# Nine tiles of a modulation as row products on VectorE in the dense layer

## The chip, the cores and the metric

The kernel runs on one core of one Trainium2 chip. A time is the device time of one execution of the whole program in microseconds, and a change is judged by the median of several executions. A profiled execution gives the span (first to last instruction) and a trace of every engine: TensorE (PE, with its weight loads as PEld), VectorE (DVE), ScalarE (ACT), GpSimd (POOL) and SyncE (SP), whose queue issues nearly all transfers.

## The reference, cut to what matters

Two layers work on 256 latent and 256 context tokens of 1024 features, all in fp32. Both layers take shifts, scales and gates from a conditioning vector `c` and from a fixed context vector `c_ctx`:

```python
s_c, s_cc = silu(c), silu(c_ctx)
for l in range(2):
    sh1, sc1, gt1, sh2, sc2, gt2 = split(s_c @ w_ada[l] + b_ada[l], 6)      # latent tokens
    sh1c, ..., gt2c              = split(s_cc @ w_ada[l] + b_ada[l], 6)     # context tokens
    h = rmsnorm(x) * (1 + sc1) + sh1
    x = x + gt1 * (mixer(h @ w_in[l]) @ w_out[l])      # pooling, conv, attention, scan
    h = rmsnorm(x) * (1 + sc2) + sh2
    x = x + gt2 * (swiglu(h) if l == 0 else top2_of_8_experts(h))
```

`w_ada[l]` is 1024 x 6144. So the modulation is two vectors of 1024 against two matrices of 25 MB each: nearly no arithmetic for its bytes. Context tokens are carried through layer 0 and only read in layer 1. The result is the latent stream after a last norm.

## The kernel before, in words

The residual lies in SBUF with features on partitions: eight tiles of 128 features x 512 tokens (`xres`). All large products are exact to fp32 by a split: a block of weights of 512 KB (`raw`, 128x1024) is rounded to a short form on ScalarE (`wh`, L277), the rest is a subtraction on VectorE (`wl`, L280), and every product is three matmuls (L559: `wh` x high, `wl` x high, `wh` x low). There are three pairs of split buffers (`NSPLIT`). All `raw` blocks go through one ring of buffers in the order of the program (`raw`, L285): five fixed ones, some more by stage (`NRAWA`, `NRAWF`, L318), and loads are all issued on SP's queue (L316).

The stages in order of time, with the start in the trace: the first mixer (0), the dense layer (283, its twenty steady blocks from 317), the second layer's norm and mixer (667), the routing to experts (834) and the experts (862). In the dense layer (`ffn`, L1114) a block `f` is 48 matmuls into two accumulators, `gps` and `ups`, from two weight blocks; then `glu` (L1125) passes it through ScalarE (tanh, L1127), two VectorE products (L1128, L1129), ScalarE and a subtraction on VectorE (L392, L393). Groups of 6, 6, 6 and 4 blocks are followed by a down projection of eight outputs (`dps`), whose results go into the residual with the gate, chunks 40 to 47 (L1108).

The modulation of a layer is twelve tiles of 512 columns, numbered 0 to 11: 0 to 3 and 6 to 9 hold shift and scale, 4 and 5 and 10 and 11 the gates. A tile (`ada`, L408) is four `raw` blocks of the matrix and eight products of a 32-column operand that holds the two vectors (sixteen matmul instructions on TensorE), four of them side by side in quarters of the array, into one accumulator `adaps` that up to four tiles share. When a group of tiles is complete, ScalarE copies the accumulator (`adaev`, L427), and at the next call eight matmuls (`adao`, L440) gather and turn it; VectorE adds the bias (`ada_out`, L447) and makes the gains. `ADAGROUPS` says which tiles form a group, and `ADAFILL` how many tiles run at each of 62 calls of `fill`, which stand after every block of the mixers and of the dense layer and in the norms and the routing. Four tiles run ahead of all that. The framework's planner orders the instructions of each engine by the program's order and estimated times; a few orders are written out by hand (`inorder`).

Of the kernel before, what the change touches and what calls it, by code (L numbers as in the profile page):

```python
# [8 lines left out]
F32 = mybir.dt.float32  # L9
F32R = mybir.dt.float32r  # L10
I32 = mybir.dt.int32
AF = mybir.ActivationFunctionType
OP = mybir.AluOpType
AX = mybir.AxisListType

P = 128
# [4 lines left out]
TCARGS = dict(schedule_with_timeline_sim=True)  # L21
NRAW = 5
NRAWA = (0, 2)
NRAWF = 10
PSB = dict(g=4, s=2, m=2)
TMPB = dict(t2=6, sd=4, sh=4, at=4)
NEARLY = 264
# [2 lines left out]
DFE = 1408  # L30
KORD = (4, 5, 6, 7, 0, 1, 2, 3)
OSLOT = ("xst", "Bt", "nab", "zs", None, None, "BT", "CT")
ADAFILL = (0, 1, 0, 1, 0, 1, 0, 1, 0, 1, 0, 1, 0, 1, 0, 1, 0, 0, 1, 1, 0, 0, 0, 2, 0, 0, 0, 0, 0, 0, 0, 0, 0, 0, 0, 0, 0, 0, 0, 0, 1, 1, 1, 0, 0, 1, 0, 0, 0, 1, 0, 0, 0, 1, 0, 0, 0, 0, 0, 0, 0, 2)
NATT = ((4, 4, 4, 4, 4, 4, 4, 4, 4, 4, 4, 4, 4, 4, 4, 4), (2, 2, 2, 2, 2, 2, 2, 2, 2, 2, 2, 2, 2, 2, 2, 2))
ATAGS = 'mmm'
G4 = 'gggg'
ADAGROUPS = ((0, (4, 5, 6, 7)), (0, (8, 9, 10, 11)), (1, (0, 1)), (1, (2, 3)), (1, (4, 5, 6)), (1, (7, 8, 9)), (1, (10, 11)))
FADA = 'm'
FGROUPS = (6, 6, 6, 4)

# [88 lines left out]
def ada_chunks():  # L129
    out = []  # L130
    for b in (0, 24):
        for j in range(4):
            out.append((b + 2 * j, b + 2 * j + 1, b + 8 + 2 * j, b + 8 + 2 * j + 1))
        for j in range(2):
            out.append(tuple(b + 16 + 4 * j + i for i in range(4)))
    return out


ADA = ada_chunks()


def pack_inputs(inp):
    g = {k: np.asarray(v) for k, v in inp.items()}
# [4 lines left out]
    out = {}  # L148
# [33 lines left out]
    q = np.arange(256)  # L182
    k = np.arange(256)
# [10 lines left out]
    ada = np.empty((2, 12, 4, P, 2, 4, P), np.float32)  # L194
    for nt, ch in enumerate(ADA):
        ada[:, nt] = wa[:, :, :, list(ch), :].reshape(2, 4, 2, P, 4, P).transpose(0, 1, 3, 2, 4, 5)
    out["ada"] = ada.reshape(2, 12, 4, P, 1024)
    wi = g["w_in"].reshape(2, 8, P, 2824)
    first = np.empty((2, 4, P, 2, 4, P), np.float32)
    for i, n in enumerate(MFIRST):  # L200
# [9 lines left out]
    wo = g["w_out"].reshape(2, 8, P, 2, 4, P)[:, list(KORD)]  # L210
# [38 lines left out]
class Kern:  # L249
# [158 lines left out]
    def ada(self, l, group, i, pool=None):  # L408


        if i == 0:
            self.adaps = self.ps(self.adatag, "adaps")
        acc = self.adaps
        w = 6 - 2 * i
        for k in range(0, 8, 2):
            t = self.raw(self.a["ada"][l, group[i], k // 2], pool=pool)
            for kk in range(2):
                g = (k + kk) % 4
                m = self.mm(acc[32 * g:32 * g + 32, :], self.s38[:, k + kk, w:w + 32], t[:, kk * 512:kk * 512 + 512],
                            start=i == 0 and k < 4, stop=k >= 4)  # L420
                if self.adaaft is not None:
                    self.inorder([self.adaaft, m])
        self.adamm = m
        if i < len(group) - 1:
            return
        ev = self.adap.tile([P, 512], F32, name="adaev")
        self.A.copy(ev, acc)  # L427
        self.pend.append((l, group, ev))

    def ada_flush(self):  # L430
        for p in self.pend:
            self.ada_end(*p)
        self.pend = []
# [680 lines left out]
    def ffn(self, l, acc, fill):  # L1114
        self.adatag = FADA
        V, A = self.V, self.A
        w0 = self.weights(self.a["fg0"][0])
        rb = self.rstd(acc, 4, fill)
        self.fill_after(fill, self.rbmm)
        for H in self.normed(l, 24, rb, "hffn"):  # L1120
            pass
        al = slice(0, T)
        acc2 = self.accp.tile([P, T], F32, name="acc")

        def glu(g, u):  # L1125
            th = self.tmp("gth")[:, :T]
            A.activation(th, g, AF.Tanh, scale=0.5)  # L1127
            V.scalar_tensor_tensor(th, th, 1.0, g, op0=OP.add, op1=OP.mult)  # L1128
            V.scalar_tensor_tensor(th, th, 0.5, u, op0=OP.mult, op1=OP.mult)  # L1129
            t = self.atp.tile([P, 2, T], F32R, tag="aT", name="aT")  # L1130
            self.hilo(t, al, th)
            return t

        pst = self.group4([self.a["fg0"][b] for b in range(4)], H, (al,) * 4, w0=w0)
        ready = [glu(pst[0], pst[1]), glu(pst[2], pst[3])]
        f, fd = 2, 0
        for gi, n in enumerate(FGROUPS):
            while len(ready) < n:
                pg, pu = self.ps("g", "gps"), self.ps(G4[2 + f % 2], "ups")
                for b in range(2):  # L1140
                    w = self.weights(self.a["fg1"][f - 2, b])
                    for kk in range(4):
                        k = b * 4 + kk
                        self.three(pg, w, kk * 256, H[k], al, k == 0, k == 7)
                        self.three(pu, w, kk * 256 + P, H[k], al, k == 0, k == 7)
                ready.append(glu(pg, pu))
                f += 1
                fill()
            idx = 0
            for d in range(8):  # L1150
                p = self.ps(DPS[d % len(DPS)], "dps")
                for i in range(n):
                    if idx % 8 == 0:
                        w = self.weights(self.a["fd"][fd])
                        fd += 1
                    self.three(p, w, (idx % 8) * P, ready[i], al, i == 0, i == n - 1)
                    idx += 1
                self.resid(l, 40, d, p, 2, acc2 if gi == len(FGROUPS) - 1 else None)
            ready = []
        return acc2  # L1160
# [738 lines left out]
    def run(self):  # L1899
        tc, nc, a = self.tc, self.nc, self.a  # L1900
        with ExitStack() as es:
            self.setup(es)
            acc = self.accp.tile([P, T], F32, name="acc")
            todo = iter([(l, g, i) for l, g in ADAGROUPS for i in range(len(g))])
            turns = iter(ADAFILL)

# [5 lines left out]
            with tc.tile_pool(name="act", bufs=8) as self.act:  # L1912
                with tc.tile_pool(name="layp", bufs=1) as self.layp:
# [26 lines left out]
                    self.load_layer(1)  # L1940
                    with tc.tile_pool(name="aTp", bufs=6) as self.atp, self.more_raw("rawf", NRAWF):
                        acc = self.ffn(0, acc, fill)
# [25 lines left out]
                self.final()  # L1968


_INS = ["shv", "consts", "xt", "lyv", "nab", "ada", "wi0", "wi1", "wi2", "wo", "fg0", "fg1", "fd", "mg0", "mg1", "md"]


# [17 lines left out]
```

## Time and profile before

| what | value |
|---|---|
| runs | 1237.04, 1235.37, 1232.88 us; median 1235.37 |
| profiled execution | 1239.41 us, span 1237.6 us, mean granted clock 0.987 |
| busy share | PE 97%, PEld 68%, DVE 53%, ACT 37%, POOL 1% |
| instructions | 18157, of them 384 matmuls of modulation tiles and 88 that gather and turn them |
| moved | 263 MB, of them 96 blocks of 512 KB of the modulation's matrices |

Busy shares of a line say how long the engine held instructions, not how well. A matmul's end is modelled, and matmuls overlap, so their pace is read from the starts. "idle before" in brackets is the time in which that engine had nothing to do, with what ended it. A group of matmuls in a timeline line has one start and a count.

### The profile page before, as it was taken

The page shows a single profiled execution, that of the slowest core. Times are in us where ns is not written, and L with a number is a line of the kernel's source. Part 1 is how long each engine was busy: PE and PEld are TensorE (multiplying, and loading weights), DVE is VectorE, ACT ScalarE, POOL GpSimd, SP SyncE. Part 2 cuts the span into 40 slices and gives each one's busy share as a digit, 9 for nine tenths or more (in the row PEclk, how much of TensorE's full clock was granted, in tenths as well). Part 3 has the DMA queues.
Part 4 walks back from the last instruction along what each step waited for, and adds up shares of the span by engine and source line. Part 5 has one row for each costly group of instructions (what it writes and reads, how often), then busy time and mean ns, then how long its engine had stood idle before and what let it go on. Part 6 is the DMA issues. An engine that isn't in the chain of part 4 may idle for free. (4 is left out here: it accounts for less than half of the span.)

```text
span 1237.6 us, 18157 instructions
## 1 busy us (share of the span) xinstructions
PE 1196.5 (97%) x6769; PEld 841.9 (68%) x6769; DVE 650.5 (53%) x1464; ACT 461.0 (37%) x864; POOL 8.9 (1%) x30
## 2 busy tenths in 40 slices
PE   6999999999999999999999999998999999999994
PEld 3787676687778888888886887894467534446741
DVE  4554557356334334434336777744478543446942
ACT  4443453224331222232223545541166333335731
POOL 0000000000000000000000000000000000000000
PEclk9999999999999999999999999998999999999998
DMA  9635413528642222222222255366999899896994
GB/s 375 229 120 205 153 69 136 209 94 329 232 147 98 96 89 99 93 95 102 87 102 101 105 206 220 116 245 231 402 397 401 323 399 396 320 397 239 339 337 171
DMA packets 87840, 263.12 MB, mean 213 GB/s; under 512 B 8128, under 2 KB 23104, under 8 KB 87744
## 3 DMA queue, kind: packets, MB, share of 16 engines
q1 hardware_dynamic: 87168, 259.79, 56.7%
q0 software_dynamic: 576, 2.10, 0.5%
q8 instruction: 55, 0.90, 0.3%
q14 instruction: 41, 0.34, 0.1%
HBM read 260.80 MB, written 1.05 MB: 212 GB/s over the span
## 5 line engine op out<-in xcount | busy, mean ns | idle before, releaser
L280 DVE TENSOR_TENSOR wl<-raw,wh 128x512 fp32r<-128x512 f32 (+2 forms) x292 | 259.6, 918 | 175.8 <-ACT wh L277 174.4
L277 ACT ACTIVATE wh<-raw 128x512 fp32r<-128x512 f32 (+2 forms) x292 | 227.2, 813 | 278.1 <-PE dps L335 80.8
L335 PE MATMUL g<-hmix,wh 128*128 128x512 f32 (+1 forms) x640 | 183.9, 366 | 0.3
L335 PEld LDWEIGHTS g<-hmix,wh 128*128 128x128 f32 x640 | 113.6, 190 | 34.0 <-issue 11.0
L335 PE MATMUL gps<-hffn,wh 128*128 128x512 f32 x320 | 125.6, 395 | 0.0
L335 PE MATMUL ups<-hffn,wh 128*128 128x512 f32 x320 | 125.5, 394 | 0.0
L335 PE MATMUL g<-hmix,wl 128*128 128x512 f32 (+1 forms) x320 | 116.2, 363 | 0.0
L335 PE MATMUL dps<-aT,wh 128*128 128x512 f32 x352 | 111.1, 394 | 0.0
L335 PE MATMUL mgu<-wh,xg 128*128 128x512 f32 (+1 forms) x288 | 90.8, 386 | 0.0
L335 PEld LDWEIGHTS dps<-aT,wh 128*128 128x128 f32 x352 | 66.0, 188 | 16.5 <-ACT wh L277 0.8
L335 PEld LDWEIGHTS gps<-hffn,wh 128*128 128x128 f32 x320 | 60.4, 189 | 14.9 <-DVE gth L1129 0.8
L335 PEld LDWEIGHTS ups<-hffn,wh 128*128 128x128 f32 x320 | 60.5, 189 | 14.2
L335 PE MATMUL dps<-aT,wl 128*128 128x512 f32 x176 | 69.6, 396 | 0.0
L335 PEld LDWEIGHTS g<-hmix,wl 128*128 128x128 f32 x320 | 60.8, 190 | 8.4 <-issue 0.9
L335 PE MATMUL ups<-hffn,wl 128*128 128x512 f32 x160 | 63.4, 396 | 0.0
L335 PE MATMUL gps<-hffn,wl 128*128 128x512 f32 x160 | 63.4, 396 | 0.0
L335 PEld LDWEIGHTS mgu<-wh,xg 128*128 128x128 f32 x288 | 53.6, 191 | 14.3 <-issue 2.9
L335 PE MATMUL mgu<-wl,xg 128*128 128x512 f32 (+1 forms) x144 | 58.1, 404 | 1.0 <-DVE wl L280 0.7
L335 PE MATMUL adaps<-raw,s 128*32 128x512 f32 x384 | 56.0, 623 | 0.0
L1108 DVE SCALAR_TENSOR_TENSOR xres<-dps,mods,xres 128x256 f32<-128x256 f32 x64 | 27.6, 478 | 43.3 <-PE dps L335 43.3
L1128 DVE SCALAR_TENSOR_TENSOR gth<-gth,gps 128x512 f32<-128x512 f32 x20 | 13.8, 688 | 62.4 <-ACT gth L1127 62.4
L335 PE MATMUL mgu<-raw,xgw 128*32 128x512 f32 (+1 forms) x340 | 45.4, 557 | 0.0
(390 smaller groups left out, 1782.5 us busy)
## 6 DMA issues: line engine op xcount, KB each, us to landing
raw<-in_mg_dram SPq DMA_DIRECT2D x142, 512.0 KB, 7.4
raw<-in_ada_dram SPq DMA_DIRECT2D x96, 512.0 KB, 4.9
raw<-in_md_dram SPq DMA_DIRECT2D x77, 512.0 KB, 7.2
raw<-in_fg_dram SPq DMA_DIRECT2D x44, 512.0 KB, 3.3
raw<-in_wi_dram SPq DMA_DIRECT2D x40, 512.0 KB, 5.4
raw<-in_fd_dram SPq DMA_DIRECT2D x22, 512.0 KB, 3.3
xres<-in_mg_dram SPq DMA_DIRECT2D x22, 512.0 KB, 7.1
raw<-in_wo_dram SPq DMA_DIRECT2D x16, 512.0 KB, 5.2
```

What stands on the lines that cost most here:

```text
L277: up = self.A.activation(h, src, AF.Copy)
L280: sub = self.V.tensor_tensor(lo, src, h.bitcast(F32), op=OP.subtract)
L335: return self.E.matmul(out, l, r, start=start, stop=stop, skip_group_check=True)
L1108: self.V.scalar_tensor_tensor(self.x[:, d, s], ps[:, s], gt[:, j:j + 1], self.x[:, d, s], op0=OP.mult, op1=OP.add)
L1128: V.scalar_tensor_tensor(th, th, 1.0, g, op0=OP.add, op1=OP.mult)
```

## The change

Nine of the twenty tiles that `fill` ran are taken off TensorE: tiles 10 and 11 of layer 0, and 2, 3 and 7 to 11 of layer 1. They are worked out in the dense layer from the rows of the transposed matrix: a block of 128 outputs x 1024 inputs has one output per partition, the two activated vectors lie repeated on all partitions (1 MB, `crep`), and one VectorE instruction multiplies and sums 1024 elements to one number per partition. A tile is four such blocks, each with two products (`c` and `c_ctx`). A generator `ada_rows` does two blocks after each `f` of the dense layer, 36 blocks in the first 18 of 20. The blocks go through the same ring, whose extra part shrinks from ten to seven, and the repeated vectors and a scratch tile take the place. `ADAFILL` and `ADAGROUPS` drop the nine tiles; calls 9 and 11 now run tiles 8 and 9 of layer 0, and the calls at 13 and 15 (first mixer), 23 (dense layer), 45, 49, 53 (second mixer) and 61 (routing) run none.

```diff
-NRAWF = 10
+NRAWF = 7
...
-ADAGROUPS = ((0, (4, 5, 6, 7)), (0, (8, 9, 10, 11)), (1, (0, 1)), (1, (2, 3)), (1, (4, 5, 6)), (1, (7, 8, 9)), (1, (10, 11)))
+ADAGROUPS = ((0, (4, 5, 6, 7)), (0, (8, 9)), (1, (0, 1)), (1, (4, 5, 6)))
+
+ADAV = ((0, 10), (0, 11), (1, 2), (1, 3), (1, 7), (1, 8), (1, 9), (1, 10), (1, 11))
...
+    wt = g["w_ada"].reshape(2, 1024, 48, P)
+    out["adat"] = np.stack([wt[l][:, list(ADA[nt]), :].transpose(1, 2, 0) for l, nt in ADAV])
+    c2 = np.stack([g["c"][0], g["c_ctx"]]).reshape(1, 2048)
+    out["crep"] = np.ascontiguousarray(np.broadcast_to(c2, (P, 2048)))
...
+    def ada_rows(self, pool):
+
+        V = self.V
+        s = pool.tile([P, 2, 1024], F32, name="srep", bufs=1)
+        sv = s.rearrange("p j k -> p (j k)")
+        self.nc.sync.dma_start(out=sv, in_=self.a["crep"])
+        y = pool.tile([P, 1024], F32, name="sprod", bufs=1)
+        for j in range(2):
+            self.A.activation(y, s[:, j], AF.Tanh, scale=0.5)
+            V.scalar_tensor_tensor(y, y, 1.0, s[:, j], op0=OP.add, op1=OP.mult)
+            V.tensor_scalar(s[:, j], y, 0.5, None, op0=OP.mult)
+        for n, (l, nt) in enumerate(ADAV):
+            o = self.persist.tile([P, 4, 2], F32, name="adar%d" % n)
+            for q in range(4):
+                t = self.raw(self.a["adat"][n, q])
+                for j in range(2):
+                    V.scalar_tensor_tensor(y, t[:, :1024], 1.0, s[:, j], op0=OP.mult, op1=OP.mult,
+                                           accum_out=o[:, q, j:j + 1])
+                if q < 3:
+                    yield
+            self.ada_out(l, nt, o)
+            yield
...
+        rows = self.ada_rows(self.atp)
         f, fd = 2, 0
...
                 fill()
+                for _ in range(2):
+                    next(rows, None)
```

## Rows read from the trace of the kernel before

**Rows 1.** The page's busy times: engine, busy us (share of the span) xinstructions.

```profile
PE 1196.5 (97%) x6769; PEld 841.9 (68%) x6769; DVE 650.5 (53%) x1464; ACT 461.0 (37%) x864; POOL 8.9 (1%) x30
```

**Rows 2.** Busy times by stage: window, its us, busy by engine, granted clock, DMA share, GB/s.

```profile
170.00:292.00 122.00, 120.85 (x605) 84.63 (x604) 63.10 (x153) 39.51 (x81) 0.00 (x0) 0.99 0.42 153
292.00:317.00 25.00, 25.00 (x120) 19.29 (x120) 19.33 (x43) 13.65 (x24) 0.00 (x0) 1.00 1.00 406
317.00:667.00 350.00, 350.00 (x1527) 281.57 (x1523) 144.60 (x200) 94.18 (x110) 0.00 (x0) 1.00 0.30 104
...
692.00:834.00 142.00, 141.55 (x1043) 122.81 (x1041) 93.40 (x231) 69.93 (x145) 3.01 (x14) 1.00 0.49 177
834.00:862.00 28.00, 24.04 (x191) 12.99 (x194) 16.10 (x92) 5.20 (x13) 0.00 (x0) 0.88 0.56 209
862.00:1195.00 333.00, 327.92 (x2157) 178.50 (x2149) 193.01 (x448) 146.90 (x307) 0.00 (x0) 0.99 0.96 361
```

**Rows 3.** Waits of TensorE's weight loads, 317 to 667: us in total, times, longest.

```profile
PEld gps L335 <- DVE gth L1129: 0.8, 1, 0.8
PEld dps L335 <- ACT wh L277: 0.8, 1, 0.8
```

**Rows 4.** The chain that ended last: start us, us, what.

```profile
1206.24 12.16 DMA raw<-in_md_dram
```

**Rows 5.** Timeline of VectorE, first mixer and dense layer: start us, us, instruction, idle before.

```profile
229.16 0.74 DVE L622 SCALAR_TENSOR_TENSOR cy<-ch,layerv,cy 128x510 f32<-128x510 f32 x1
...
340.11 0.69 DVE L1128 SCALAR_TENSOR_TENSOR gth<-gth,gps 128x512 f32<-128x512 f32 x1 [2.84 <-ACT gth L1127]
...
341.50 1.22 DVE L280 TENSOR_TENSOR wl<-raw,wh 128x1024 fp32r<-128x1024 f32 x1
342.64 0.69 DVE L393 TENSOR_TENSOR aT<-gth,aT 128x512 fp32r<-128x512 f32 x1
346.92 1.23 DVE L280 TENSOR_TENSOR wl<-raw,wh 128x1024 fp32r<-128x1024 f32 x1 [3.60 <-ACT wh L277]
351.27 0.69 DVE L1128 SCALAR_TENSOR_TENSOR gth<-gth,gps 128x512 f32<-128x512 f32 x1 [3.12 <-ACT gth L1127]
```

**Rows 6.** Timeline of TensorE at the end of the first dense group.

```profile
362.06 0.40 PE L335 MATMUL ups<-hffn,wh 128*128 128x512 f32 x1
362.39 1.92 PE L335 MATMUL adaps<-raw,s 128*32 128x512 f32 x16
364.24 0.50 PE L335 MATMUL dps<-aT,wh 128*128 128x512 f32 x1
```

**Rows 7.** Timeline of TensorE in the second mixer.

```profile
784.48 0.95 PE L335 MATMUL adao<-constp,adaev 128*128 128x6 f32 x8
785.29 0.37 PE L335 MATMUL g<-hmix,wh 128*128 128x256 f32 x1
```

**Rows 8.** Timeline of all engines, 311 to 320.

```profile
315.74 1.92 PE L335 MATMUL adaps<-raw,s 128*32 128x512 f32 x16
...
316.44 1.28 DVE L1129 SCALAR_TENSOR_TENSOR gth<-gth,g 128x512 f32<-128x512 f32 x2
...
317.59 0.19 PEld L335 LDWEIGHTS gps<-hffn,wh 128*128 128x128 f32 x1 [0.84 <-DVE gth L1129]
```

**Rows 9.** Timeline of all engines in the routing.

```profile
834.90 3.64 PE L335 MATMUL adaps<-raw,s 128*32 128x512 f32 x32
...
839.91 0.17 DVE L1252 TENSOR_TENSOR emask<-topm,topm 128x16 fp32r<-128x16 f32 x1
...
840.40 0.36 PE L335 MATMUL rank<-emask,rones 128*128 128x8 f32 x2 [1.86 <-ACT ge L1322]
```

**Rows 10.** Groups of instructions by line and form: count, busy us, mean ns, idle before.

```profile
L280 DVE TENSOR_TENSOR wl<-raw,wh 128x1024 fp32r<-128x1024 f32 x122 | 149.1, 1223 | 152.9 <-ACT wh L277 152.0 <-DMA raw<-in_wo_dram 0.7
...
L756 DVE TENSOR_REDUCE nm<-attsb 128x1 f32<-128x512 f32 x16 | 10.9, 680 | 0.2
```

**Rows 11.** Timeline of ScalarE, dense layer and second mixer.

```profile
345.83 1.06 ACT L277 ACTIVATE wh<-raw 128x1024 fp32r<-128x1024 f32 x1 [3.58 <-PE ups L335]
...
753.51 0.22 ACT L757 ACTIVATION_READ_ACCUMULATOR attP<-attsb,nm 128x1 f32 x1
```

More of the change, by code (lines that the diff above doesn't have):

```diff
@@ L32 @@
 OSLOT = ("xst", "Bt", "nab", "zs", None, None, "BT", "CT")
-ADAFILL = (0, 1, 0, 1, 0, 1, 0, 1, 0, 1, 0, 1, 0, 1, 0, 1, 0, 0, 1, 1, 0, 0, 0, 2, 0, 0, 0, 0, 0, 0, 0, 0, 0, 0, 0, 0, 0, 0, 0, 0, 1, 1, 1, 0, 0, 1, 0, 0, 0, 1, 0, 0, 0, 1, 0, 0, 0, 0, 0, 0, 0, 2)
+ADAFILL = (0, 1, 0, 1, 0, 1, 0, 1, 0, 1, 0, 1, 0, 0, 0, 0, 0, 0, 1, 1, 0, 0, 0, 0, 0, 0, 0, 0, 0, 0, 0, 0, 0, 0, 0, 0, 0, 0, 0, 0, 1, 1, 1, 0, 0, 0, 0, 0, 0, 0, 0, 0, 0, 0, 0, 0, 0, 0, 0, 0, 0, 0)
 NATT = ((4, 4, 4, 4, 4, 4, 4, 4, 4, 4, 4, 4, 4, 4, 4, 4), (2, 2, 2, 2, 2, 2, 2, 2, 2, 2, 2, 2, 2, 2, 2, 2))
@@ L1968, in moe_over @@
                 self.final()
-_INS = ["shv", "consts", "xt", "lyv", "nab", "ada", "wi0", "wi1", "wi2", "wo", "fg0", "fg1", "fd", "mg0", "mg1", "md"]
+_INS = ["shv", "consts", "xt", "lyv", "nab", "ada", "adat", "crep", "wi0", "wi1", "wi2", "wo", "fg0", "fg1", "fd", "mg0", "mg1", "md"]
 def kernel(**inputs):
```

## Prediction

> **What bounds the kernel now.** I read the page's busy times first, then the busy times by stage, the waits of TensorE's weight loads, and last the timelines around the places that the change touches. The page puts TensorE at 97% and VectorE at 53% [rows 1]. The page's share is an average, so the stages decide: TensorE is busy for 120.85 of 122 us at the end of the first mixer, for all 350 us of the dense layer and for 141.55 of 142 us in the second mixer, while VectorE works 144.60 of the 350 us [rows 2]. In the dense layer the loads of weights wait twice, 0.8 us each, outside the modulation itself [rows 3]. So up to 834 us TensorE's instruction stream is the path, and whatever leaves it comes off the end, if nothing new has to be waited for. The expert stage (862 to 1195) has TensorE busy 327.92 of 333 us and the DMA engines at 0.96; it ends with a wait of 12.16 us for one load of the down projection [rows 2, 4].
>
> **What the change removes.** Nine tiles go, each of sixteen 32-column matmuls, and three of the seven groups' closing products (tiles 2 and 3, 7 to 9, 10 and 11 of layer 1). The price of a tile: an iteration of the dense layer has 48 matmuls in 351.27 - 340.11 = 11.16 us, 0.2325 us each [rows 5]. The last matmul ahead of a tile starts at 362.06, so the next would start at 362.29; with the tile between it starts at 364.24: 1.95 us [rows 6]. A closing product takes from 784.48 to 785.29, 0.8 us, and delays its successor a little: 0.85 us [rows 7].
>
> In the first mixer it is tiles 10 and 11 of layer 0: 2 x 1.95 = 3.9 us, on a TensorE that is busy throughout [rows 2].
>
> In the dense layer it is tiles 2 and 3 of layer 1 with their closing product. The second stands alone on TensorE [rows 6]: 1.95, and 0.85 for the closing product. The first lies between the opening four blocks and the next gate product, which waited for VectorE's L1129 [rows 8]. If the buffer it needs is the one L1129 frees (first of two done at about 317.1), only 0.5 us is gained; if it is one freed earlier, 1.9. I take 1.0. Together 3.8.
>
> In the second mixer it is tiles 7 to 9 of layer 1 and a closing product: 3 x 1.95 + 0.85 = 6.7 us.
>
> In the routing it is tiles 10 and 11 of layer 1. Both run from 834.90 while VectorE works towards the expert mask at 839.91, and the ranks start only at 840.40 [rows 9]. Nothing is gained on TensorE. The granted clock of 834 to 862 is already 0.88 [rows 2]; TensorE will now be idle for 3.6 us more ahead of the ranks, whose products would at worst take twice their 0.7 us. Some additions leave VectorE's chain there (a few tenths). Between -0.4 and +0.7; I take 0.
>
> Sum removed: 3.9 + 3.8 + 6.7 = 14.4 us. The mixers' tiles also filled small gaps between attention and the scan; if each of the five there left a fifth of itself behind as a wait, that is 2 us, if none 0. I take 1.0: 13.4 us.
>
> **What it adds.** 72 products 128x1024 with a running sum on VectorE, 36 loads of 512 KB and one of 1 MB on SP's queue, two tanh on ScalarE and four operations on VectorE to prepare the vectors.
>
> The trace has no VectorE operation that sums its result, so it is bounded. Below: the two-operand subtraction of 1024 takes 1223 ns [rows 10] and frees VectorE 1.14 us after its start (341.50 to 342.64 [rows 5]). A multiplication with addition whose two tensors both lie in SBUF takes 0.74 us at 510 elements, about the same pace [rows 5]. Above: product and sum as two passes, 1.14 and a reduction: 680 ns at 512 [rows 10], so about 1.2 at 1024, together 2.34. On ScalarE a sum costs one more short instruction of 0.22 us [rows 11], and that is the nearest row in kind: I take 1.14 and a little under 0.2, 1.3 us, 94 us in all, and keep 1.14 and 2.34 as ends.
>
> Against this stands the Trainium skill, Vector Engine (DVE) Microarchitecture Reference, section Points that are easy to get wrong: an instruction of this kind (two tensors and a scalar) with two SBUF sources that aren't bf16 runs at half throughput, since both read ports are taken and none is left for the accumulator. The row of 0.74 us disagrees for an instruction without a sum; no row shows one with it. By the rule a product would take an estimated 2.3 us or a little more; that is the first rival below.
>
> Does that fit? In an iteration VectorE is idle 3.60 + 3.12 = 6.72 of 11.16 us [rows 5]. Two row blocks with two products each (one for each vector) take 4 x 1.3 = 5.2 us. They fit, with 1.5 us over. The whole layer: 144.6 + 94 of 350 us, 68%. The order on VectorE is fixed, so a product can sit in front of something TensorE needs. The subtraction for a weight block has time: with three pairs of split buffers a block may be split once the third before it is used, two blocks (11.16 us) ahead of need; from the release at 345.8 to its end at 348.15 [rows 5, 11] takes 2.4, so 8.8 us are left, seven products. The tight place is the end of a group of dense blocks: the last gated block passes ScalarE, two multiplications, ScalarE and a subtraction, and the down projection uses it 15 matmuls (3.5 us) after it starts. Each of the three groups with row products may lose up to two products there (2.6 us); at best nothing. I take 0.5 each, 1.5 us. If that cover is gone altogether, it costs 7.8.
>
> The preparation is about 4.6 us on VectorE and 2.1 on ScalarE, while the window 292 to 317 leaves VectorE 25 - 19.33 = 5.7 idle [rows 2]; at nothing, and up to 4 if it lands in front of the normalization. The sums with the bias are the same small additions as before, only earlier.
>
> The dense layer loads eight modulation blocks already; 28 are new there, and 1 MB. 104 GB/s over 350 us is 36 MB; with 15.7 MB more it is some 150 GB/s, where the stage before moved 406 [rows 2]. The ring of buffers goes from 15 to 12, three iterations of four loads each or 33 us ahead. On SP's queue every new load stands behind a load of the same iteration, so nothing is passed that is needed sooner; the 1 MB comes in the one full stretch (share 1.00), some 2.6 us at 406 GB/s, ahead of blocks that are needed only after 317. At nothing; a block that came late all the same would cost what it is late, and show as a wait of ScalarE's copy for a load. The mixers lose 20 loads from their small rings of five and seven.
>
> In the expert stage eight loads fewer stand ahead of the weights, so up to eight more of its blocks can be there when it starts. It is paced by TensorE with only 333 - 327.92 = 5 us idle [rows 2], so at most 5 us is won; but the ring's position at its start moves, and with it which buffer the last loads wait for, where 12.16 us lies open [rows 4]: a loss of 3 us is as thinkable. I take 0.
>
> **Sum.** -13.4 + 1.5 = -11.9 us. Against the profiled execution, 1239.41 us (span 1237.6), that is 1227.5, or -0.96%. The profiled execution lies 4.0 us above the median of the runs, 1235.37; the same share off the median gives 1223.5 us.
>
> **Rivals.**
> First, VectorE becomes the bound in the dense layer (slower). At 2.34 us an iteration needs 9.36 where 6.72 are idle: 2.64 too many. With 8.8 us of lead per group, groups of 4, 6 and 6 such iterations stall 1.8 + 7.0 + 7.0 = 15.8 us, and the ends of groups 2 us each: 22 us against 13.4, so 1235.4 + 8.5 = 1244. It decides from about 2.2 us per product. For it: no row shows the sum. Against: the VectorE rows shown go at one pace, and part of the products may run during the down projections, where VectorE idles more.
>
> Second, the hand-offs take it. Products in front of the gated block cost the full 7.8 us and the gaps of the mixers 2: 14.4 - 9.8 = 4.6, 1231. For: a fixed order laid out ahead by estimated times. Against: VectorE has 1.5 us over per iteration and the block's subtraction gives way by microseconds.
>
> Third, the expert stage gains as well, its weights being further ahead: 5 us more, 1218.5. For: DMA at 0.96. Against: TensorE hardly waits there.
>
> Fourth, the preparation arrives late, so that products wait in order on VectorE for the 1 MB load and block subtractions behind them: its 4 us and some, 1228.
>
> **Chances.** Forecast 0.62 (own range 1217 to 1229), rival 1 0.10, rival 2 0.12, rival 3 0.10, rival 4 0.06. About 0.3% (3.7 us) is what a measurement of this kernel tells from no change. Rivals 3 and 4 and two thirds of rival 2 are faster by more than that (1231 lies beyond 1231.7), the rest of it the same: faster 0.82, same 0.07, slower 0.11. The range 1213 to 1237 leaves out most of rival 1 and a little on the other side.
>
> **What will show it.** In the changed profile: 72 products on VectorE at about 1.2 us with a short second instruction; at 2.3 rival 1 holds. In the dense layer TensorE's weight loads still wait for hardly anything; waits for L1128, L1129 or L393 at the starts of the down projection mean rival 2, waits for the subtraction of weights rival 1. Dense layer shorter by about 2 us, second mixer by 6 to 7, first mixer by 3 to 4, routing unchanged, expert stage 375 us from 862 to the end as before. The prediction is wrong if the mixers keep their length, if the dense layer grows, or if the expert stage moves by more than 5 us.

## The result, and the profile after

The changed kernel takes 1214.26 us (median of four runs, 1213.07 to 1215.84) beside 1235.12 for the kernel before: ratio 0.9833, 95% interval 0.9812 to 0.9853, 20.9 us faster. The forecast was 11.9 us, 1223.5. The direction is right, and the time lies in the stated range of 1213 to 1237, by 1.3 us; it lies outside the forecast's own range (1217 to 1229) and beyond rival 3's 1218.5. The gain is 1.75 times the sum, so the question is where nine more microseconds came from.

The page's busy times (engine, busy us, share, instructions) and its line for the products (busy, mean ns, then idle time before them and what ended it):

```profile
PE 1165.6 (96%) x6601; PEld 831.0 (69%) x6601; DVE 736.8 (61%) x1612; ACT 461.1 (38%) x863; POOL 8.9 (1%) x30
...
L453 DVE SCALAR_TENSOR_TENSOR sprod<-raw,srep 128x1024 f32<-128x1024 f32 x72 | 87.8, 1220 | 26.3 <-DMA raw<-in_adat_dram 25.8
```

TensorE is busy for 31 us less than in [rows 1], VectorE for 86 more. The products cost 1.22 us and not 2.3. VectorE's timeline in the first down projection shows what one occupies:

```profile
374.19 1.22 DVE L453 SCALAR_TENSOR_TENSOR sprod<-raw,srep 128x1024 f32<-128x1024 f32 x1
375.33 0.08 DVE L453 DVE_READ_ACCUMULATOR sprod<-raw,srep 128x1 f32 x1
375.45 1.22 DVE L453 SCALAR_TENSOR_TENSOR sprod<-raw,srep 128x1024 f32<-128x1024 f32 x1
```

From one product's start to the next one's it is 1.26 us; I had taken 1.3. (Another instruction mostly starts together with the read, 1.15 us after the product.) By the Trainium skill (Vector Engine (DVE) Microarchitecture Reference, Points that are easy to get wrong) it should have been an estimated twice that; the trace disagrees for two fp32 sources with a sum.

The busy times by stage that answer to [rows 2] (window, its us, then busy by PE, PEld, DVE, ACT and POOL, granted clock, DMA share, GB/s):

```profile
170.00:283.00 113.00, 111.61 (x554) 81.12 (x552) 59.97 (x143) 38.05 (x77) 0.00 (x0) 0.98 0.37 130
283.00:307.00 24.00, 23.50 (x108) 18.88 (x104) 22.35 (x46) 14.16 (x25) 0.00 (x0) 1.00 0.98 394
307.00:653.00 346.00, 345.73 (x1488) 280.17 (x1488) 227.86 (x360) 94.15 (x110) 0.00 (x0) 1.00 0.44 148
...
680.00:814.00 134.00, 131.92 (x983) 119.47 (x981) 93.34 (x226) 68.83 (x145) 3.01 (x14) 1.00 0.36 127
814.00:841.00 27.00, 19.30 (x157) 11.29 (x161) 15.81 (x84) 4.51 (x11) 0.00 (x0) 0.81 0.60 222
```

In the dense layer VectorE is busy for 228 of 346 us, TensorE for all of them. TensorE's weight loads wait once, where [rows 3] has two waits:

```profile
PEld gps L342 <- DVE gth L1158: 1.2, 1, 1.2
```

Nothing waits for a hand-off at the end of a group: that fear was unfounded.

To compare stages I read where the first matmul of each stage starts: `vps`, `g<-hffn` (the dense layer), the last start of `dps` (its end), `logits` (the routing), `rank` (the ranks) and `mdn<-wh,aT` (the first down product of the experts' full pass). The first profile of before is a poor base: besides the stretches shown later it has two at half clock (a granted clock of 0.50, TensorE's lower level of 1.2 GHz), at 150 to 158 and 286 to 292 us, which a second profile of the same kernel lacks; that one has a span of 1234.2 instead of 1237.6. The one at 150 costs 3.2 us (19.95 us from one group of `yps` to the next, against 16.75); the one at 286 costs nothing that shows, and the changed kernel has its like at 276 to 282. So I set the changed kernel against the second profile. Lengths in us:

| stage | before, 1st | before, 2nd | changed | difference to 2nd | forecast |
|---|---|---|---|---|---|
| start to `vps` | 47.8 | 48.8 | 48.0 | -0.8 | 0 |
| first mixer | 244.5 | 241.5 | 235.0 | -6.5 | -3.5 |
| dense layer | 373.9 | 373.9 | 370.0 | -3.9 | -2.3 |
| second norm and mixer | 153.9 | 153.8 | 146.9 | -6.9 | -6.1 |
| routing to the ranks | 20.3 | 20.3 | 20.0 | -0.3 | 0 |
| ranks to first `mdn<-wh,aT` | 108.7 | 109.4 | 102.7 | -6.7 | 0 |
| from there to the end | 288.5 | 286.5 | 288.7 | +2.2 | 0 |
| sum | 1237.6 | 1234.2 | 1211.3 | -22.9 | -11.9 |

(The forecast's 1.0 us for gaps is dealt out over the five tiles of the mixers. The start varies from run to run, 47.7 to 49.1, so its 0.8 us are no gain. The two profiles differ by 22.9 us, the medians by 20.9. "Before again" below is the second profile of before.)

### The profile page after: what moved, and what is told of

Read it like the earlier page. It is cut to its first block, busy times and chain, and to the rows that moved or that the text cites. A ratio compares the mean times of both kernels' runs of the same rounds, so it can differ in the third digit from the quotient of the medians.

```text
span 1211.3 us, 17942 instructions
## 1 busy us (share of the span) xinstructions
PE 1165.6 (96%) x6601; PEld 831.0 (69%) x6601; DVE 736.8 (61%) x1612; ACT 461.1 (38%) x863; POOL 8.9 (1%) x30
## 5 line engine op out<-in xcount | busy, mean ns | idle before, releaser
L287 DVE TENSOR_TENSOR wl<-raw,wh 128x512 fp32r<-128x512 f32 (+2 forms) x288 | 257.0, 920 | 108.9 <-ACT wh L284 108.0
L453 DVE SCALAR_TENSOR_TENSOR sprod<-raw,srep 128x1024 f32<-128x1024 f32 x72 | 87.8, 1220 | 26.3 <-DMA raw<-in_adat_dram 25.8
L1663 DVE SCALAR_TENSOR_TENSOR mth<-mth,mgu 128x256 f32<-128x256 f32 (+1 forms) x30 | 11.5, 394 | 53.2 <-ACT mth L1662 52.8
L342 PE MATMUL mdn<-wh,aT 128*128 128x512 f32 x132 | 43.5, 400 | 0.0
```

What stands on the lines that cost most here:

```text
L287: sub = self.V.tensor_tensor(lo, src, h.bitcast(F32), op=OP.subtract)
L342: return self.E.matmul(out, l, r, start=start, stop=stop, skip_group_check=True)
L453: V.scalar_tensor_tensor(y, t[:, :1024], 1.0, s[:, j], op0=OP.mult, op1=OP.mult, accum_out=o[:, q, j:j + 1])
L1663: V.scalar_tensor_tensor(th, th, 1.0, p[:, :hw], op0=OP.add, op1=OP.mult)
```

## The experiments

**The parts alone.** Four kernels move one stage's tiles to row products and leave the others on TensorE; all four pay for the 1 MB load, the preparation and the smaller ring. Edits, against the kernel before with the change's code:

```diff
 # e1_first: calls 13 and 15 run none
+ADAV = ((0, 10), (0, 11))
 # e2_dense: call 23 runs none
+ADAV = ((1, 2), (1, 3))
 # e3_second: calls 45, 49 and 53 run none
+ADAV = ((1, 7), (1, 8), (1, 9))
 # e4_routing: call 61 runs none
+ADAV = ((1, 10), (1, 11))
```

> Only tiles 10 and 11 of layer 0 go from the first mixer to row products (8 of them blocks, 16 products); the other seven stay on TensorE where they were. Theory A (the prediction's sum): two tiles of 1.95 us leave the first mixer and nothing else changes, 3.4 to 3.9 us faster than before. Rival B (the two traces laid side by side, where 207 to 283 us shrank by 6.2): about 6 us faster. Both expect nothing of the expert stage, since ScalarE's order there is as before: none of its weight conversions (wh) stands ahead of the first tanh of a 128x256 gate (mth<-mgu) after the gathers.

> Only tiles 2 and 3 of layer 1 go from the dense layer to row products. Theory A: 1.0 + 1.95 + 0.85 us leave TensorE, less up to 0.5 for a hand-off at a group's end: 3.3 to 3.8 us faster. Rival B (a tile at the opening of the layer was wholly hidden behind the wait for L1129, and the closing product lay in a gap): 2 us faster. Expert stage unchanged in both; ScalarE has no conversion ahead of the tanh of 128x256 there, as before.

> Only tiles 7 to 9 of layer 1 go from the second mixer to row products. Theory A: three tiles and a closing product, 6.7 us faster, expert stage unchanged. Rival C (the expert stage's gain comes from the order on ScalarE, which the planner lays out by its estimate of the loads): here four weight conversions stand ahead of the tanh of 128x256 in the expert stage (none before, six in the changed kernel), so TensorE finds its first weights ready, the 3.4 us at the lower clock at 905 us go, and the expert stage is 4 to 5 us shorter: 11 to 12 us faster in all. Rival D (the lower clock at 905 us in the profile of before was a matter of that one execution): 6.7 us faster, with the expert stage shorter by at most 2.

> Only tiles 10 and 11 of layer 1 go from the routing to row products. Theory A (the prediction): nothing, between 0.4 faster and 0.7 slower. Rival C: six weight conversions stand ahead of the tanh of 128x256 in the expert stage, as in the changed kernel, so 5 to 6 us faster, all of it between 848 and 950 us. Rival D: within 2 us of before, with the waits for wl and wh at 902 to 905 us gone but no more.

Measured against before on the same chip, and stage lengths from each profile ("us faster" is worked out from the ratio; the difference of the medians is 4.4, 2.3, 7.8 and 1.6 us for the four parts):

| kernel | ratio (95%) | us faster | first mixer | dense | second | ranks to `mdn` | ranks to end |
|---|---|---|---|---|---|---|---|
| before again | | | 241.5 | 373.9 | 153.8 | 109.4 | 395.9 |
| e1_first | 0.9950 (0.9931 to 0.9968) | 6.2 | 235.0 | 374.5 | 153.8 | 106.8 | 397.1 |
| e2_dense | 0.9969 (0.9954 to 0.9985) | 3.8 | 241.4 | 370.0 | 153.8 | 106.1 | 394.2 |
| e3_second | 0.9924 (0.9907 to 0.9941) | 9.4 | 241.4 | 374.5 | 147.2 | 105.1 | 394.9 |
| e4_routing | 0.9982 (0.9968 to 0.9996) | 2.2 | 241.4 | 374.6 | 153.8 | 103.7 | 394.6 |
| changed | 0.9833 (0.9812 to 0.9853) | 20.9 | 235.0 | 370.0 | 146.9 | 102.7 | 391.4 |

Up to the ranks the parts add up: each stage shrinks in the kernel that takes its tiles out, and in no other. The intervals are some 2 us to either side, so this rests on the stage lengths. The first mixer's two tiles are worth 6.5 us and not 3.9 (rival B). Theory A holds for e2_dense. In e3_second the stage gives 6.6 and from the ranks to the end 1.0 is won: rival D, not the 4 to 5 of rival C. e4_routing, 2.2 us faster (0.5 to 3.9), is just beyond theory A's 0.4 and short of rival C. The dense pair is worth 3.9 to 4.5. In the three kernels that leave it in place the dense layer is 0.6 longer; the timeline of TensorE shows why in e4_routing:

```profile
359.01 0.40 PE L342 MATMUL ups<-hffn,wh 128*128 128x512 f32 x1
359.33 3.64 PE L342 MATMUL adaps<-raw,s 128*32 128x512 f32 x32
362.91 0.50 PE L342 MATMUL dps<-aT,wh 128*128 128x512 f32 x1
```

The planner put both tiles of the pair behind the first group (32 matmuls, where [rows 6] has 16). The one at the opening had cost 1.1 us there, behind the wait for L1129 [rows 8], and costs 1.7 here. The row products themselves cost this layer nothing that shows: behind that place the starts of the gated blocks stand at the same distance from before's through all groups.

**The split's order in the expert stage (e6_split_late).** Before, ScalarE converts no weight ahead of the first tanh of 128x256 in the expert stage; in the changed kernel it converts six blocks' halves there, so they are ready when TensorE comes. The edit puts them back behind the tanh:

```diff
-                A.activation(th, p[:, :hw], AF.Tanh, scale=0.5)
+                ta = A.activation(th, p[:, :hw], AF.Tanh, scale=0.5)
+                if last and nt == 0:
+                    self.alead = ta   # weight conversions after this one
```

> The changed kernel with one order added: ScalarE's weight conversions of the first full expert come after the tanh of 128x256 (mth<-mgu), as in the kernel before; six of them stood ahead of it. Theory C: the expert stage loses what it had won, TensorE waits for wl and wh at its first full weights, 3 to 5 us slower than the changed kernel, so about 16 to 18 us faster than before. Rival D: no difference to the changed kernel (within 1 us), 21 us faster than before.

1215.34 us, ratio 0.9840 (0.9814 to 0.9866), 19.8 us faster than before: within 1.1 us of the changed kernel. The waits of the weight loads over 870 to 890 us show that the edit did what it says; first this kernel, then the changed one:

```profile
PEld mgu L342 <- ACT wh L284: 1.8, 2, 1.2
...
PEld mgu L342 <- DVE wl L287: 1.4, 3, 0.8
```

```profile
PEld mgu L342 <- DVE wl L287: 0.4, 1, 0.4
```

Counted from the ranks, the first weight products come 1.4 to 2.1 us later, yet `mdn<-wh,aT` starts 102.0 us after the ranks, not 102.7: TensorE's other products of that stretch fill in. My theory C falls as the cause of the gain.

**The kernel before once more (e5_before_again)**, unchanged, one profile.

> The kernel before, profiled once more. Theory D (the stretches at the lower clock at 150 and 905 us in its first profile belong to that one execution): both are missing, the span is 3 to 5 us shorter than 1237.6, and from the ranks to the first down product of the full pass (mdn<-wh,aT) it takes 107 us instead of 108.7, as in the kernel with only the first mixer's tiles moved (106.8). Theory C (the order of work makes the stretch at 905): it is there again, with TensorE's waits for wl and wh at 902 to 905 us, and 108 to 109 us between the two points.

1236.02 us, span 1234.2. The stretches at 150 and 286 us are gone. The one at 905 is there again, with 109.4 us between the two points, as C had it; D had the one at 150 right and this one wrong. TensorE's timeline there and the busy times of the stretch (the granted clock is the third number from the end), two blocks for before again and two for e1_first:

```profile
903.38 0.73 PE L335 MATMUL mgu<-wl,xg 128*128 128x512 f32 x1 [0.74 <-DVE wl L280]
903.91 1.05 PE L335 MATMUL mgu<-wh,xg 128*128 128x512 f32 x2
904.77 0.63 PE L335 MATMUL mgu<-wl,xg 128*128 128x512 f32 x1
```

```profile
901.00:909.00 8.00, 7.26 (x24) 5.24 (x25) 7.17 (x12) 6.27 (x12) 0.00 (x0) 0.79 1.04 403
```

```profile
895.99 0.50 PE L342 MATMUL mgu<-wl,xg 128*128 128x512 f32 x1 [0.73 <-DVE wl L287]
896.33 0.63 PE L342 MATMUL mgu<-wh,xg 128*128 128x512 f32 x2
896.79 0.39 PE L342 MATMUL mgu<-wl,xg 128*128 128x512 f32 x1
```

```profile
893.50:899.00 5.50, 4.71 (x19) 3.33 (x20) 5.50 (x10) 5.44 (x12) 0.00 (x0) 1.00 1.04 402
```

The same wait, 0.74 and 0.73 us, is followed by half clock in one (three products in 1.39 us) and by full clock in the other (0.80). By the granted clock in slices of 2 us it costs before an estimated 1.7 us. Both profiles of before have it. The kernel e12_whole below, edited in the first mixer alone, hasn't, and takes 106.2 us between the two points. So with all tiles on TensorE this stretch already varies from 106.2 to 109.4 us, and the 6.7 of the table is measured from its upper end.

**VectorE's room (e7_double, e11_quad).** Each product two or four times:

```diff
                 for j in range(2):
-                    V.scalar_tensor_tensor(y, t[:, :1024], 1.0, s[:, j], ...)
+                    for _ in range(2):   # e11_quad: range(4)
+                        V.scalar_tensor_tensor(y, t[:, :1024], 1.0, s[:, j], ...)
```

> The changed kernel with each of the 72 products done twice (the second overwrites the first): 2.5 us instead of 1.26 for a block and a vector, what rival 1 of the prediction feared, though in two instructions. The prediction's sum for such a price: an iteration needs 10.1 us where 6.7 are idle, the three groups fall behind by 5 to 13 us each, some 30 us slower than the changed kernel and slower than before. The other view (the planner puts the products where VectorE is idle, in the down projections too, where it has some 20 of 33 us free): VectorE's 180 + 144 of 350 us still fit, and it is at most 5 us slower than the changed kernel, so still 16 us faster than before.

> The changed kernel with each of the 72 products done four times (5.0 us for a block and a vector). VectorE then has 72 x 5.0 = 360 us beside its 145 in 350 us of dense layer. Rival 1 of the prediction, VectorE as the bound, must show here: some 150 us slower than the changed kernel, with TensorE waiting for the weight subtractions. If the time is still the same, the products don't stand on the path at all, whatever they cost.

Doubled: 1214.27 us, ratio 0.9838 (0.9808 to 0.9867); the dense layer is 369.9 us, as with single products. Four times: 1367.07 us, ratio 1.1066 (1.1037 to 1.1095), 153 us slower than the changed kernel. Busy times of the dense layer, doubled and then four times:

```profile
307.00:653.00 346.00, 345.60 (x1487) 280.10 (x1488) 309.88 (x504) 94.50 (x111) 0.00 (x0) 1.00 0.46 148
```

```profile
307.00:806.00 499.00, 379.96 (x1560) 296.91 (x1560) 469.31 (x780) 95.87 (x115) 0.00 (x0) 0.86 0.32 105
```

At 310 of 346 us on VectorE TensorE waits once, 1.2 us, as with single products; beyond its capacity the whole excess shows, as worked out (150). The waits aren't where I expected them: in the dense layer of the fourfold kernel, up to 653 us, TensorE's loads wait 64.9 us for ScalarE's conversions and 4.2 for the subtractions. What saves the doubled kernel is the planner: its last product starts at 614.6 instead of 554.8, and many run in the down projections (from 563 to 586 us, inside the third, products take 10.7 us of VectorE, with single products none). So VectorE would become the bound near an estimated (346 - 145) / 72 = 2.8 us for a product; no run lies between 2.5 and 5.0. The prediction's rival 1 decided from 2.2, since it gave the products only the iterations and 8.8 us of lead.

**More tiles (e8_fourteen, e10_ten).** Fourteen: all of layer 1 and tiles 10 and 11 of layer 0. Ten: the nine and tile 4 of layer 1.

```diff
 # e8_fourteen
+ADAV = ((0, 10), (0, 11), (1, 0), ..., (1, 11))
+                for _ in range(3 if f < 7 else 2):
+                    next(rows, None)
+                if d % 2 and gi < 3:      # in the down projections
+                    next(rows, None)
 # e10_ten
+ADAV = ((0, 10), (0, 11), (1, 2), (1, 3), (1, 4), (1, 7), ..., (1, 11))
```

> All twelve tiles of layer 1 and the last two of layer 0 as row products: 56 blocks, three after each of the first four iterations of the dense layer, two after the others, and one after every second output of the first three down projections. Five more tiles and two closing products leave TensorE: 5 x 1.95 + 2 x 0.85 = 11.4 us at most; three of the tiles stand in the second layer's norm, where TensorE is idle for 0.7 of 25 us and partly waits for the norm, so 5 to 11 us faster than the changed kernel if TensorE alone counts. If the 20 more products (50 us of VectorE in all with 40 of them) come in the way of the weight subtractions, or the norm's gap only opens, no gain.

> The changed kernel with a tenth tile, tile 4 of layer 1, as row products (40 blocks, two after each of the 20 iterations). Of the three tiles at the second layer's norm one ran ahead of the norm's sums (653.31 to 655.17), two inside its waits. If the one ahead is what goes and the two still fill the waits: 1.9 us faster than the changed kernel, about 22.8 faster than before. If the planner leaves a wait open instead, as in the kernel with fourteen, no difference, within 1 us.

Fourteen: 1214.32 us, 0.9841 (0.9815 to 0.9867), nothing beyond nine. TensorE's timeline at the norm ahead of the dense layer and the busy times of 16 us there, two blocks for this kernel and two for the changed one:

```profile
279.54 2.07 PE L342 MATMUL rbc<-constp,rsy 128*128 128x128 f32 x8 [2.44 <-DVE rsy L394]
284.05 0.80 PE L342 MATMUL g<-hffn,wh 128*128 128x512 f32 x1 [2.44 <-ACT hffn L574]
284.64 0.63 PE L342 MATMUL g<-hffn,wl 128*128 128x512 f32 x1
```

```profile
275.00:291.00 16.00, 10.22 (x39) 8.37 (x39) 11.80 (x30) 7.94 (x13) 0.00 (x0) 0.68 0.99 394
```

```profile
276.62 2.96 PE L342 MATMUL adaps<-raw,s 128*32 128x512 f32 x16
279.50 1.75 PE L342 MATMUL rbc<-constp,rsy 128*128 128x128 f32 x8
281.19 1.92 PE L342 MATMUL adaps<-raw,s 128*32 128x512 f32 x16
283.04 0.51 PE L342 MATMUL g<-hffn,wh 128*128 128x512 f32 x1
```

```profile
274.00:290.00 16.00, 15.10 (x89) 9.95 (x89) 11.52 (x33) 7.64 (x14) 0.00 (x0) 0.89 0.95 377
```

Taking tiles 0 and 1 away opens two waits of 2.44 us in which they had run, and the first weight products then go at half clock: counted from `vps`, the dense layer's steady part (`gps`) starts 1.8 us later. At the second layer's norm the three tiles are as free: that stage is 147.2 us beside 146.9. Ten: 1212.76 us, 0.9814 (0.9795 to 0.9834), the fastest of all, but its interval overlaps the changed kernel's and its norm and mixer take 147.1: not shown to be better.

**The routing pair put back (e9_seven)**: the nine less tiles 10 and 11 of layer 1.

```diff
+ADAV = ((0, 10), (0, 11), (1, 2), (1, 3), (1, 7), (1, 8), (1, 9))
```

> The changed kernel with tiles 10 and 11 of layer 1 back on TensorE at the routing; seven tiles stay as row products. The prediction's sum: no difference to the changed kernel, 21 us faster than before. Rival C (the pair and its eight loads are what the expert stage gained): 4 to 5 us slower than the changed kernel, the stage from the ranks to the first down product of the full pass back at 107 to 109 us instead of 102.7. Rival E (the parts add up as alone, where the pair gave 2.2 us): 2 us slower than the changed kernel, about 18.7 us faster than before.

1216.39 us, 0.9851 (0.9829 to 0.9874), 18.4 us faster: by the medians the pair is worth some 2 us, as alone, though the interval overlaps the changed kernel's. From the ranks it takes 104.1 us to `mdn<-wh,aT`, not 107 to 109, and e7_double with all nine has 104.0: nearest rival E, and against C.

**The cut tiles (e12_whole).** In the kernel before the two tiles of the first mixer don't run in one piece. TensorE's timeline of before again, with another cut tile at 133 us ahead of them:

```profile
133.19 1.06 PE L335 MATMUL adaps<-raw,s 128*32 128x512 f32 x8
134.19 1.12 PE L335 MATMUL attS<-kT,qT 64*128 64x512 f32 x2
135.24 1.07 PE L335 MATMUL adaps<-raw,s 128*32 128x512 f32 x8
136.24 0.50 PE L335 MATMUL g<-hmix,wh 128*128 128x512 f32 x1
...
212.29 0.40 PE L335 MATMUL g<-hmix,wh 128*128 128x512 f32 x1
212.62 1.05 PE L335 MATMUL adaps<-raw,s 128*32 128x512 f32 x2
213.59 0.70 PE L335 MATMUL attS<-kT,qT 64*128 64x256 f32 x2
214.22 1.92 PE L335 MATMUL adaps<-raw,s 128*32 128x512 f32 x14
216.07 0.50 PE L335 MATMUL g<-hmix,wh 128*128 128x512 f32 x1
...
229.77 0.40 PE L335 MATMUL g<-hmix,wh 128*128 128x512 f32 x1
230.10 1.92 PE L335 MATMUL adaps<-raw,s 128*32 128x512 f32 x14
231.95 0.44 PE L766 MATMUL attT<-constp,attP 128*128 128x128 f32 x2
232.32 1.04 PE L335 MATMUL adaps<-raw,s 128*32 128x512 f32 x2
233.29 0.50 PE L335 MATMUL g<-omx,wh 128*128 128x512 f32 x1
```

Fourteen take from 214.22 to 216.07, about as long as sixteen in [rows 6], and the two left over another 0.97. From the `g` ahead to the `g` behind it is 3.78 and 3.52 us; less that product's own 0.23 and what the attention pair costs elsewhere (0.72 and 0.15 by its neighbours' starts), a tile costs 2.8 and 3.1 us instead of 1.95: 2.0 more for the two. It is the place of the cut that costs: two matmuls alone hold the engine for 0.97 us, eight for 1.00 (133.19 to 134.19), so 2 and 14 take 2.82 us, but 8 and 8 only 2.00, beside 1.85 for sixteen in one piece. The Trainium skill (TensorEngine Tiling (Array Packing), Tiling Modes) says that a change of the tiling mode drains the engine. The tile cut 8 and 8 has such changes too and takes only 0.15 us more, so here the drain is at most a small part of the price. The edit keeps attention out of the two tiles:

```diff
+                if l == 0 and group[i] > 9 and k + kk == 0 and self.attlast is not None:
+                    self.inorder([self.attlast, m])     # after the attention products so far
...
+            if self.tilelast is not None:
+                self.inorder([self.tilelast, ms[0]])    # later attention products behind the tile
```

> The kernel before with one order added: in the first mixer no attention product comes between the matmuls of tile 10 or of tile 11 of layer 0 (before, one ran as 2 and 14, the other as 14 and 2 with attention products between). Nothing leaves TensorE. Theory F (a tile that is cut so costs 2.8 to 3.1 us instead of 1.95, since two matmuls alone take as long as four side by side, and that is why the first mixer gained 6.4 and not 3.9): about 2 us faster than before, all of it between 205 and 240 us. Rival G (the extra gain came from elsewhere in the mixer, such as fewer loads on the small ring): no difference, within 0.5 us between the same points.

1241.29 us, 1.0041 (1.0026 to 1.0056), slower. The planner now ran both tiles side by side and late, and TensorE's weight loads waited for their blocks (190 to 292 us; 3.2 of the 8.8 us by which this stage grew are, besides, the half clock at 150 to 158 us, there again in this profile):

```profile
PEld adaps L336 <- DMA raw<-in_ada_dram: 4.7, 3, 2.4
PEld g L336 <- ACT wh L278: 2.5, 1, 2.5
```

So it tests something else than it meant to, and the price of the cut rests on the timeline, not on an experiment. It does show that a tile's place in this mixer, with five buffers for its loads, can cost more than the tile.

## Why the prediction was right, and where its size was off

The mechanism held, and with it the direction; that the time still lies in the stated range, by 1.3 us, is in part luck, since the terms below all erred to the same side. Right: TensorE's stream is the path up to the ranks; 1.26 us for a product (1.3); room on VectorE; nothing for the 1 MB load and the preparation (rival 4: no); the second mixer's three tiles and closing product (6.7, measured 6.6 to 6.9).

The terms that were mis-sized:

- **Two tiles of the first mixer at 1.95 us.** That price was read in the dense layer, where a tile runs whole [rows 6]. In the mixer both are cut 2 and 14. Measured 6.5 for the pair (e1_first); the timeline accounts for 5.9, the rest is open.
- **Hand-offs, 1.5 us, and gaps, 1.0.** Neither is there. The dense layer gave 3.9, which is the gross 3.8 of the sum; the planner put products where VectorE was idle, and doubling them changed nothing.
- **Routing at 0.** TensorE idles ahead of the ranks as foreseen, and no loss from the clock shows, which I had feared. TensorE's timeline at the ranks and the busy times of the twelve us at half clock, two blocks for before again and two for the changed kernel:

```profile
832.84 3.64 PE L335 MATMUL adaps<-raw,s 128*32 128x512 f32 x32
838.34 0.35 PE L335 MATMUL rank<-emask,rones 128*128 128x8 f32 x2 [1.86 <-ACT ge L1322]
...
838.92 1.85 PE L335 MATMUL adao<-constp,adaev 128*128 128x4 f32 x8
```

```profile
838.00:850.00 12.00, 9.79 (x52) 7.38 (x52) 8.60 (x48) 0.00 (x0) 0.00 (x0) 0.57 0.14 45
```

```profile
819.91 0.56 PE L342 MATMUL rank<-emask,rones 128*128 128x8 f32 x2 [5.14 <-ACT ge L1355]
```

```profile
816.00:828.00 12.00, 5.53 (x28) 4.56 (x28) 11.02 (x58) 2.58 (x5) 0.00 (x0) 0.57 0.40 139
```

  Both have the same mean clock there, but in the changed kernel the half clock starts during the idle time and covers 5.5 us of work, before 9.8. And I had left out the pair's closing product, 1.85 us at that clock, between the ranks and the gathers: these start 3.56 to 4.30 us after the ranks in the seven profiles with the pair at the routing, and 3.54 to 3.56 in the six without. By `atr<-stack`, some 18 us on, the changed kernel is 2.1 us further ahead than at the ranks. That is one execution against one: over all profiles it is 18.3 to 19.9 us with the pair and 17.8 to 19.1 without, 0.6 less in the mean, so most of the 2.1 is not shown to be the pair's.
- **Expert stage at 0.** From the ranks to the end it is 4.5 us shorter, net; rival 3 had 5 us for it, with a chance of 0.10. This is the step that failed, the largest term put at nothing. The net gain holds beyond the one pair of profiles: three with all tiles on TensorE take 397.2, 395.9 and 395.8 us (before twice, e12_whole), three with nine off 391.4, 391.0 and 392.4 (changed, e6_split_late, e7_double), 4.7 less in the mean. Where in the stage it arises is not shown. By the second profile of before, 6.7 us are won up to `mdn<-wh,aT` and 2.2 lost behind it; by e12_whole it is 3.5, and behind it nothing is lost (289.6 us, changed 288.7). Of the 6.7 an estimated 1.7 are the stretch at half clock at 905. The earlier conversions would account in place for some 2, but e6_split_late took these back without losing the time, so that cause is not shown. The parts alone win between -1.2 and 1.7 us net here, 2.8 together, and all nine 4.5; profiles with all tiles on TensorE differ by 1.4. So it stays open whether the parts add up or the loads ahead do something together; after the ranks 130.5 MB are still moved, before 133.6.

Rival 1 was put wrongly, not only unlikely: at 2.5 us a product, more than its 2.34, nothing happens. The profiled execution's 4 us above the median were scaled away; by e5_before_again most of them (3.2) were the stretch at half clock at 150 to 158 us, ahead of every tile that the change moves. The chances were added up wrongly: forecast, rivals 3 and 4 and two thirds of rival 2 make 0.86 for faster, with 0.04 for the same and 0.10 for slower.

## What to carry to other kernels

Read an instruction group's price in the stage where it runs: the same sixteen matmuls cost 1.95 us in one piece, some 3 when cut 2 and 14, and nothing where they fill a wait; there, taking them out was even followed by a lower clock (0.68 for 0.89 over 16 us). An engine at 66% with a planner that moves work into its idle stretches could take products of twice the price for nothing; at four times the price the sum over the stage was more than full, and all of the excess showed. Profile the kernel before more than once: two executions of it differed by 3.4 us of span, most of it a stretch at half clock far from the change, and a gain of 2 us in one stage of one pair of profiles was within what profiles with the same work there differ by.

## What the hardware showed unexpectedly

A multiplication of two fp32 tensors in SBUF with a running sum (128x1024) took 1.22 us and a 0.08 us read of the sum, 1.26 from start to start, no slower than the 1.22 of a plain subtraction [rows 10]. The same wait of TensorE of 0.73 to 0.74 us was followed by half clock in one kernel and by full clock in another, with the same instructions around it. Two 32-column matmuls alone held TensorE for 0.97 us, eight for 1.00, fourteen for 1.85.
